# Second block: value products of a whole head per key block, probabilities left unnormalised, and their reciprocals multiplied into the gate

## The chip, the cores and the metric

The kernel runs on one core of one Trainium2 chip. The metric is the device time of one execution in microseconds. The kernel before was timed three times: 941.24, 942.96 and 945.05 us, median 942.96 us. Engines are named as in the profile: PE is TensorE, DVE is VectorE, ACT is ScalarE, POOL is GpSimd, and SP is the queue that issues the DMAs.

## The reference

One sequence of 512 positions and 1024 columns goes through two blocks. The first is retention and differential attention; the change does not touch it. The second has sixteen heads of 64 value columns: eight "a" heads (dilated windows, three patterns, here folded into one biased softmax over 512 keys) and eight "b" heads (latent attention, causal). Each head's output is normalised by its softmax sum, gated, and projected:

```
def dilated_pattern(q, k, v, rel_bias, window, dilation):
    ...
    m = jnp.max(s, axis=-1, keepdims=True)
    p = jnp.exp(s - m)
    den = jnp.sum(p, axis=-1)
    ...
    o = jnp.einsum('bnrhqk,bnkrhd->bnqrhd', p, vw) / den_q[..., None]

def latent_attention(...):
    ...
        p = jax.nn.softmax(s, axis=-1)
        return jnp.einsum('bhqk,bkhd->bqhd', p, v)

def hybrid_layer(...):
    ...
    mixed = jnp.concatenate([o_a * jax.nn.silu(z_a), o_b * jax.nn.silu(z_b)], axis=-1)
    out = jnp.matmul(mixed, w_out.astype(jnp.float32))
    return (x.astype(jnp.float32) + out).astype(x.dtype)
```

## The kernel before, in words

Every dense operand is held as a high part (rounded to fp32r) and a low part (the rest), and a product is three matmuls: high by high, low by high, high by low (mm3, lines 308 to 310). The high part is a copy on ACT, the low part a subtraction on DVE (split, lines 270 and 271). For streamed weights (Streamer, lines 138 and 140) the subtraction is on DVE, or on POOL for the keys in POOL_LO.

The attention of the second block walks 64 steps: 16 heads in the order a0 to a3, b0 to b7, a4 to a7, and four query tiles t of 128 positions each. Step s does this, in the order in which the PE instructions are written (PE runs in that order; the other engines' queues are ordered by a scheduler):
- probs(s): scores of query tile t against its t+1 key blocks, a score minimum on DVE (L1115), the exponential with its sum on ACT (L1118), the reciprocal of the sum and the scaling of the row by it on DVE (L1120, L1121);
- at t = 1 and t = 2 the queries and keys of the head four steps on are transposed and stacked (ready_q, ready_k); their tiles come from a ring of 12 (QK_BUFS), 6 for a pair of a heads, 4 for a b head;
- fill: dense work of the block (gates z, projections u, q, k, v, and the last projection "wo2") is dealt out so that PE has something to do while DVE and ACT work;
- probs_T(s - 2): the t+1 blocks of the row tile of two steps ago are transposed on PE (ppt), split into high (pTh, ACT) and low (pTl, DVE);
- fill again;
- weigh(s - 3): value products. For each of the t+1 key blocks three matmuls with 64 weight columns (v of this head, high or low) and 128 moving columns (one query tile of the transposed probabilities), all into one 64x512 PSUM tile per head (oTp). After t = 3 ACT copies it (osb, L1147), and after every second head mix_in multiplies by the gate (mtmp, L1153) and splits the result (mixh, mixl) for the last projection, L1185 to L1194.

PSUM: two tiles for the transposes (ps_t), two for the scores, three for dense work, one for the value products. A table of relative biases (tb) comes back from DRAM for every a head. The loop over steps is L1252 to L1262.

Of the kernel before, what the change touches and what calls it, by code (L numbers as in the profile page):

```python
# [11 lines left out]
F32 = mybir.dt.float32  # L12
# [8 lines left out]
S = 512  # L21
# [29 lines left out]
POOL_LO = frozenset(FILL)  # L51

QK_BUFS = 12
P_BUFS = 4
# [102 lines left out]
def two_block_kernel(ctx: ExitStack, tc: tile.TileContext, A: dict, out: bass.AP):  # L157
# [123 lines left out]
    def stack_q(pool, src, col):  # L281
        out = []
        for own, other in halves:
            t = pool.tile([P, S], F32R, name="qst", tag="qk", bufs=QK_BUFS)
# [6 lines left out]
    def stack_k(pool, src):  # L291
        out = []
        for own, other in halves:
            hi = pool.tile([P, S], F32R, name="ksh", tag="qk", bufs=QK_BUFS)
            lo = pool.tile([P, S], F32R, name="ksl", tag="qk", bufs=QK_BUFS)
# [609 lines left out]
    with tc.tile_pool(name="work2", bufs=2) as wp, tc.tile_pool(name="work2c", bufs=1) as wp1:  # L905
# [19 lines left out]
        for tp in range(2):  # L925
            cn = wp.tile([P, 2, 256], F32, name="cn", tag="tb")
            ck = wp.tile([P, 2, 160], F32, name="ck", tag="p", bufs=4)
# [62 lines left out]
        def mla_kv(half, out):  # L990
            (kh, kl), = st.get(f"ukv{half}")
            k = wp.tile([P, NT, 4, 96], F32, name="mk", tag="tm", bufs=4)
            vh = wp.tile([P, NT, 4, 64], F32R, name="mvh", tag="vh")
            vl = wp.tile([P, NT, 4, 64], F32R, name="mvl", tag="vl")
            for tt in range(NT):
# [3 lines left out]
                split(vh[:, tt], vl[:, tt], ps[:, :, 64:128])  # L999
# [11 lines left out]
            out.append((k, vh, vl))  # L1011

        def mla_prep(nm, src, h):
# [3 lines left out]
            hi = wp.tile([P, S], F32R, name=nm + "h", tag="qk", bufs=QK_BUFS)  # L1017
            lo = wp.tile([P, S], F32R, name=nm + "l", tag="qk", bufs=QK_BUFS)
# [35 lines left out]
        def dil_v(g):  # L1054
            vh = wp.tile([P, NT, 256], F32R, name="avh", tag="vh")
            vl = wp.tile([P, NT, 256], F32R, name="avl", tag="vl")

            def done(tp, ps):
                split(vh[:, 2 * tp : 2 * tp + 2, :], vl[:, 2 * tp : 2 * tp + 2, :], ps)

            yield from dense_TM_steps(st.get(f"v_a{g}"), done)
            v_a[g] = (vh, vl)

        def dil_prep(nm, i):
# [3 lines left out]
            return stack_q(wp, flat(pt), gcol[:, 18:19]) if nm == "q_a" else stack_k(wp, flat(pt))  # L1068
# [27 lines left out]
        def values_of(kind, h):  # L1096
            if kind == "b":
                _, vh, vl = kv_b[h // 4]
                return vh[:, :, h % 4, :], vl[:, :, h % 4, :]
            vh, vl = v_a[h // 4]  # L1100
            cv = slice(64 * (h % 4), 64 * (h % 4) + 64)
            return vh[:, :, cv], vl[:, :, cv]

        def probs(kind, h, t):
# [8 lines left out]
            p = wp.tile([P, S], F32, name="p", tag="p", bufs=4)  # L1113
# [182 lines left out]
```

## Time and profile before

| | |
|---|---|
| median of three runs | 942.96 us |
| profiled execution: its time / its span | 943.44 us / 941.4 us |
| PE busy | 918.0 us (98%), 5109 matmuls |
| DVE busy | 557.1 us (59%) |
| ACT busy | 452.8 us (48%) |
| POOL busy | 207.6 us (22%) |
| granted TensorE clock, mean | 0.993 of full speed |

PE's busy share is an upper reading: the ends of pipelined matmuls are modelled, so the distance between two starts tells what one costs. The attention of the second block runs from about 709 to 925 us. The shares of the whole span say little about it, so the rows below take it by stretch.

### The profile page before, as it was taken

The numbers are of one execution on the slowest core, as the hardware profiler recorded it, in microseconds if no ns is written. First come the engines' busy times: TensorE is split into PE (matmuls) and PEld (weight loads), VectorE is DVE, ScalarE is ACT, GpSimd is POOL, SyncE is SP. The second block draws the span as 40 slices with busy tenths as digits, with TensorE's granted clock in tenths as the row PEclk, the third lists the DMA queues.
The fourth block names the chain that finished last, engine by engine and source line by source line (L and its number), as shares of the span: only waits on it lengthen the run. The fifth ranks groups of instructions, "written<-read, shape, count | busy, mean of one in ns | idle before, by whom it ended". The sixth has DMA issues, their size and how long they took to land.

```text
span 941.4 us, 13693 instructions
## 1 busy us (share of the span) xinstructions
PE 918.0 (98%) x5109; PEld 778.2 (83%) x5109; DVE 557.1 (59%) x1222; ACT 452.8 (48%) x923; POOL 207.6 (22%) x234
## 2 busy tenths in 40 slices
PE   8999999999999999999999999999998989999998
PEld 5788887777888888888888888888997778999886
DVE  5434332428764655667765445444649897678884
ACT  5322231235555645666565432233546667666650
POOL 2001100107110223312310000032248453341100
PEclk8999999999999999999999999999999999999999
DMA  5575031211434433222432224544323221211412
GB/s 207 140 232 172 23 112 45 89 41 49 137 121 135 130 128 90 90 85 63 136 115 66 86 90 156 172 137 146 103 83 96 56 80 46 68 46 46 155 47 90
DMA packets 70241, 96.72 MB, mean 103 GB/s; under 512 B 5351, under 2 KB 46199, under 8 KB 70176
## 3 DMA queue, kind: packets, MB, share of 16 engines
q1 hardware_dynamic: 70176, 95.86, 32.6%
q8 instruction: 40, 0.66, 0.3%
q14 instruction: 25, 0.20, 0.1%
HBM read 87.43 MB, written 11.03 MB: 105 GB/s over the span
## 4 chain that ended last, share of the span: by engine, by line
PE 87%; DVE 6%; DMA 3%; ACT 2%; POOL 1%; issue 1%; SPq 0%; ACTq 0%
PE dps L308 9%; PE dps L310 9%; PE dps L309 9%; PE tps L308 7%; PE tps L310 7%; PE tps L309 7%; PE aps L308 2%; PE aps L309 2%; PE aps L310 2%; DMA wr<-in_w_in_dram 2%; PE dop L719 2%; PE ppt L1127 2%; PE ops L308 2%; PE yps L310 2%; PE yps L308 2%; PE yps L309 2%
## 5 line engine op out<-in xcount | busy, mean ns | idle before, releaser
L140 DVE TENSOR_TENSOR wl<-wr,wh 128x1024 fp32r<-128x1024 f32 (+2 forms) x115 | 141.8, 1234 | 117.7 <-ACT wh L138 113.8
L138 ACT ACTIVATE wh<-wr 128x1024 fp32r<-128x1024 f32 (+1 forms) x132 | 137.7, 1043 | 153.0 <-DMA wr<-in_w_in_dram 53.2
L308 PE MATMUL dps<-h1h,wh 128*128 128x512 f32 x320 | 128.3, 401 | 0.0
L310 PE MATMUL dps<-h1h,wl 128*128 128x512 f32 x320 | 125.1, 392 | 0.0
L309 PE MATMUL dps<-h1l,wh 128*128 128x512 f32 x320 | 125.0, 390 | 0.0
L308 PE MATMUL tps<-wh,h1h 128*128 128x512 f32 x256 | 104.5, 409 | 4.9 <-ACT dqn L387 2.5
L310 PE MATMUL tps<-wh,h1l 128*128 128x512 f32 x256 | 103.0, 403 | 0.0
L309 PE MATMUL tps<-wl,h1h 128*128 128x512 f32 x256 | 102.0, 399 | 0.3 <-DVE wl L140 0.2
L310 PEld LDWEIGHTS dps<-h1h,wl 128*128 128x128 f32 x320 | 60.1, 188 | 13.1
L308 PEld LDWEIGHTS dps<-h1h,wh 128*128 128x128 f32 x320 | 60.1, 188 | 12.3 <-ACT vv L491 0.5
L309 PEld LDWEIGHTS dps<-h1l,wh 128*128 128x128 f32 x320 | 60.2, 188 | 11.4
L308 PEld LDWEIGHTS tps<-wh,h1h 128*128 128x128 f32 x256 | 49.1, 192 | 17.4 <-ACT dqn L387 4.2
L309 PEld LDWEIGHTS tps<-wl,h1h 128*128 128x128 f32 x256 | 49.0, 191 | 11.1 <-DVE wl L140 1.6
L310 PEld LDWEIGHTS tps<-wh,h1l 128*128 128x128 f32 x256 | 49.0, 191 | 10.9 <-DVE h1l L271 0.3
L308 PE MATMUL aps<-wh,h2h 128*128 128x256 f32 x192 | 56.9, 296 | 0.0
L309 PE MATMUL aps<-wl,h2h 128*128 128x256 f32 x192 | 54.2, 282 | 0.0
L310 PE MATMUL aps<-wh,h2l 128*128 128x256 f32 x192 | 54.2, 282 | 0.0
L140 POOL TENSOR_TENSOR wl<-wr,wh 128x1024 fp32r<-128x1024 f32 (+2 forms) x17 | 38.1, 2245 | 38.7 <-ACT wh L138 31.0
L690 DVE CUSTOM_DVE_ANT_0 p<-sp,tb 128x128 f32<-128x128 f32 (+3 forms) x64 | 29.0, 488 | 29.4 <-PE sp L305 29.3
L1118 ACT ACTIVATE p<-p,nm 128x128 f32<-128x128 f32 (+1 forms) x64 | 35.7, 557 | 21.9 <-DVE nm L1115 21.6
L693 ACT ACTIVATE p<-p,nm 128x128 f32<-128x128 f32 (+3 forms) x64 | 35.5, 556 | 15.0 <-DVE nm L690 14.7
L253 POOL TENSOR_TENSOR gnrs<-gnrs,mhalf 128x8 f32<-128x8 f32 x24 | 41.8, 1748 | 1.7
(288 smaller groups left out, 2202.0 us busy)
## 6 DMA issues: line engine op xcount, KB each, us to landing
wr<-in_w_in_dram SPq DMA_DIRECT2D x92, 512.0 KB, 3.6
wr<-in_w_out_dram SPq DMA_DIRECT2D x16, 512.0 KB, 3.9
wr<-in_ret_w_o_dram SPq DMA_DIRECT2D x8, 512.0 KB, 3.4
wr<-in_diff_w_o_dram SPq DMA_DIRECT2D x8, 512.0 KB, 3.7
rep_dram<-rev_dram SPq DMA_DIRECT2D x8, 320.0 KB, 5.3
y_dram<-my SPq DMA_DIRECT2D x8, 256.0 KB, 2.0
my<-y_dram SPq DMA_DIRECT2D x8, 256.0 KB
m_dram<-mth SPq DMA_DIRECT2D x8, 256.0 KB, 3.3
```

Source lines behind the costliest of these rows:

```text
L138: nc.scalar.activation(hi, raw, AF.Copy)
L140: eng.tensor_tensor(lo, raw, hi.bitcast(F32), op=ALU.subtract)
L253: nc.gpsimd.tensor_tensor(dst, dst, mhalf[:, :n], op=ALU.pow)
L308: nc.tensor.matmul(ps, lh, rh, start=start, stop=False)
L309: nc.tensor.matmul(ps, lh, rl, start=False, stop=False)
L310: nc.tensor.matmul(ps, ll, rh, start=False, stop=stop)
L690: nc.vector.tensor_tensor_reduce(p[:, :n], sp[:, :n], tables[head][:, S - n : S], scale=-1.0, scalar=3.0e38, op0=ALU.add, op1=ALU.min, acc ...
L693: nc.scalar.activation(p[:, :n], p[:, :n], AF.Exp, scale=-1.0, bias=nm, accum_out=den)
L719: nc.tensor.matmul(o_ps[:, t, :], aT[:, kt, :], vd[head // 4][:, kt, hc], start=kt == 0, stop=kt == t)
L1118: nc.scalar.activation(p[:, :n], p[:, :n], AF.Exp, scale=-1.0, bias=nm, accum_out=den)
L1127: nc.tensor.transpose(pt[:, kt, :], p[:, kt * P : (kt + 1) * P], ident)
```

## The change

Where the kernel before multiplies per query tile, the kernel after waits for a head's four tiles and multiplies per key block. The high and low halves of v lie side by side in one tile of 128 columns per head, so one matmul gives both products, the high one in PSUM rows 0 to 63, the low one in rows 64 to 127; it runs once with the high and once with the low part of the probabilities, over all query tiles that see the key block (512, 384, 256, 128 columns). The transposed probabilities of a head are laid out so that these columns lie together (13 blocks, two tiles per head). ACT copies rows 64 to 127 out, DVE adds them to rows 0 to 63.

The rows of probabilities are no longer scaled. The four sums of a head are gathered, doubled, inverted and written to DRAM; they come back as a row of 512 spread over 64 partitions, and for every pair of heads POOL multiplies the gate by the two rows. Besides, the low parts of the weights wo2_0 and wo2_1 move from DVE to POOL, the ring of query and key tiles in this block has 9 tiles instead of 12, that of the row tiles p 3 instead of 4, and a doubling in the query norm of the b heads goes.

```diff
-POOL_LO = frozenset(FILL)
+POOL_LO = frozenset(FILL + ("wo2_00", "wo2_01", "wo2_10", "wo2_11"))
+QK_BUFS2 = 9
...
                 ss = stat.tile([P, 8], F32, name="uss", tag="uss")
...
-                nc.vector.tensor_scalar(ss[:, 4:8], ss[:, 4:8], 2.0, None, op0=ALU.mult)
                 rs = stat.tile([P, 8], F32, name="urs", tag="urs")
-                rstd(rs, ss, 8, 1.0 / 64)
+                for c4, w in ((slice(0, 4), 64), (slice(4, 8), 32)):
+                    nc.gpsimd.tensor_scalar(rs[:, c4], ss[:, c4], 1.0 / w, EPS, op0=ALU.mult, op1=ALU.add)
+                nc.gpsimd.tensor_tensor(rs, rs, mhalf[:, :8], op=ALU.pow)
...
-                split(vh[:, tt], vl[:, tt], ps[:, :, 64:128])
+                split(v[:, tt, :, 0:64], v[:, tt, :, 64:128], ps[:, :, 64:128])
...
-            p = wp.tile([P, S], F32, name="p", tag="p", bufs=4)
+            p = wp.tile([P, S], F32, name="p", tag="p", bufs=3)
...
-            den = stat.tile([P, 1], F32, name="den", tag="den")
-            nc.scalar.activation(p[:, :n], p[:, :n], AF.Exp, scale=-1.0, bias=nm, accum_out=den)
-            rd = stat.tile([P, 1], F32, name="rd", tag="rd")
-            nc.vector.reciprocal(rd, den)
-            nc.vector.tensor_scalar(p[:, :n], p[:, :n], rd, 0.5, op0=ALU.mult, op1=ALU.mult)
+            if t == 0:
+                den_now[0] = stat.tile([P, NT], F32, name="den4", tag="den4")
+            den = den_now[0]
+            nc.scalar.activation(p[:, :n], p[:, :n], AF.Exp, scale=-1.0, bias=nm, accum_out=den[:, t : t + 1])
+            if t == NT - 1:
+                nc.vector.tensor_scalar(den, den, 2.0, None, op0=ALU.mult)
+                rd = stat.tile([P, NT], F32, name="rd", tag="rd")
+                nc.vector.reciprocal(rd, den)
+                nc.sync.dma_start(rd_dram[h // 2 + (4 if kind == "b" else 0), h % 2].rearrange("t p -> p t"), rd)
             return p
...
         def probs_T(p, t):
+            if t == 0:
+                pT_now[:] = [wp.tile([P, 13, P], F32R, name=f"pT{a}", tag="pT") for a in "hl"]
             pt = ps_t.tile([P, NT, P], F32, name="ppt", tag="t")
...
+            to = slice(t, 4 * t + 1, 3)
+            split(pT_now[0][:, to, :], pT_now[1][:, to, :], pt[:, : t + 1, :])
...
-        def weigh(kind, h, t, pT):
...
-            for i in range(t + 1):
-                mm3(o_ps[0][:, cq], vh[:, i, :], vl[:, i, :], pT[0][:, i, :], pT[1][:, i, :], i == 0, i == t)
-            if t == NT - 1:
-                j = h % 2
-                nc.scalar.activation(o_sb[kt][64 * j : 64 * j + 64, :], o_ps[0], AF.Copy)
+        def weigh(kind, h, pT):
...
+            for i in range(NT):
+                for a in range(2):
+                    nc.tensor.matmul(o_ps[:, i * P :], v[:, i, :], flat(pT[a][:, 4 * i : 3 * i + 4, :]),
+                                     start=i == 0 and a == 0, stop=i == NT - 1 and a == 1)
+            j = h % 2
+            half = wp.tile([64, S], F32, name="ohalf", tag="th", bufs=1)
+            nc.scalar.activation(half, o_ps[64:128], AF.Copy)
+            nc.vector.tensor_tensor(o_sb[kt][64 * j : 64 * j + 64, :], o_ps[0:64], half, op=ALU.add)
+            if j == 0:
+                rdb[kt] = wp.tile([P, S], F32, name="rdb", tag="rdb", bufs=1)
+            nc.sync.dma_start(rdb[kt][64 * j : 64 * j + 64, :],
+                              rd_dram[kt, j].rearrange("t p -> (t p)")[None, :].to_broadcast([64, S]))
+            if j == 1:
+                mix_in(kt)

         def mix_in(kt):
+            nc.gpsimd.tensor_tensor(zws[kt], zws[kt], rdb.pop(kt), op=ALU.mult)
             tmp = wp.tile([P, S], F32, name="mtmp", tag="th", bufs=1)
             nc.vector.tensor_tensor(tmp, zws[kt], o_sb[kt], op=ALU.mult)
...
             fill(s, 0.5)
+            if s > LAG:
+                pT = pT_of.pop(s - LAG - 1)
+                if steps[s - LAG - 1][2] == NT - 1:
+                    weigh(*steps[s - LAG - 1][:2], pT)
             if 0 <= s - LAG < n_steps:
                 pT_of[s - LAG] = probs_T(p_of.pop(s - LAG), steps[s - LAG][2])
             fill(s, 1.0)
-            if s > LAG:
-                weigh(*steps[s - LAG - 1], pT_of.pop(s - LAG - 1))
```

Lines of the kernel after stand 1 to 20 lines further down than the same lines before. Up to the first value matrix of the second block the order on all engines is the same.

PE before, where the fifth b head's value products of the first query tile stand ahead of the sixth's first scores (aps is dense work, sp are scores; names with numbers are weight tiles):

```order
L308 MATMUL aps<-wh_0_7823,h2h 128x256
L309 MATMUL aps<-wl_0_7824,h2h 128x256
L310 MATMUL aps<-wh_0_7823,h2l 128x256
L308 MATMUL oTp<-pTh,mvh 64x128
L309 MATMUL oTp<-pTl,mvh 64x128
L310 MATMUL oTp<-pTh,mvl 64x128
L308 MATMUL sp<-kh,qh 128x128
L309 MATMUL sp<-kl,qh 128x128
L310 MATMUL sp<-kh,ql 128x128
```

PE after, at the place where a b head's whole product now stands, behind the first half of the step's dense work and ahead of the next transpose (ppt):

```order
L310 MATMUL aps<-wl_1_7572,h2h 128x256
L311 MATMUL aps<-wh_1_7571,h2l 128x256
L1155 MATMUL oTp<-pTh,mv 128x512
L1155 MATMUL oTp<-pTl,mv 128x512
L1155 MATMUL oTp<-pTh,mv 128x384
L1155 MATMUL oTp<-pTl,mv 128x384
L1155 MATMUL oTp<-pTh,mv 128x256
L1155 MATMUL oTp<-pTl,mv 128x256
L1155 MATMUL oTp<-pTh,mv 128x128
L1155 MATMUL oTp<-pTl,mv 128x128
L1139 MATMUL ppt<-ident,p 128x128
L309 MATMUL aps<-wh_1_7571,h2h 128x256
```

The three short products ahead of the scores are gone, as are those of the three other tiles; eight long ones stand once per head, and the score matmuls follow dense work.

DVE before, in the b heads (L1115 is the score minimum with its read-out, L1120 and L1121 the reciprocal and the scaling, zw a gate, ql a query's low part):

```order
L1115 ISA p,nm<-sp,dist 128x128
L1115 ISA nm 128x1
L384 SCALAR_TENSOR_TENSOR zw<-gth,zps 128x512
L1120 RECIPROCAL rd<-den 128x1
L271 TENSOR_TENSOR pTl<-ppt,pTh 128x384
L1121 TENSOR_SCALAR p<-p,rd 128x128
L1115 ISA p,nm<-sp,dist 128x256
L1115 ISA nm 128x1
L275 SCALAR_TENSOR_TENSOR ql<-mpt,gcol,qh 96x512
L1120 RECIPROCAL rd<-den 128x1
L1121 TENSOR_SCALAR p<-p,rd 128x256
```

DVE after, at the end of a pair of b heads (L1118 is the score minimum there, osb the sum of the two halves, mtmp the gated output, kl a key's low part, mv a value's):

```order
L1009 TENSOR_TENSOR mk<-mk,rrs 128x4x64
L272 TENSOR_TENSOR mv<-ups,mv 128x4x64
L1160 TENSOR_TENSOR osb<-oTp,ohalf 64x512
L272 TENSOR_TENSOR pTl<-ppt,pTh 128x128
L1171 TENSOR_TENSOR mtmp<-zw,osb 128x512
L1118 ISA p,nm<-sp,dist 128x512
L1118 ISA nm 128x1
L1006 TENSOR_REDUCE rss<-usq 128x4
L272 TENSOR_TENSOR mixl<-mtmp,mixh 128x512
```

The reciprocal and the scaling have left the steps; the sum of the halves and the gated output stand in front of the next score minimum.

POOL before, around the first weights of v_a1 (gnrs is a norm, wl a weight's low part):

```order
L252 TENSOR_SCALAR gnrs<-gns 128x8
L253 TENSOR_TENSOR gnrs<-gnrs,mhalf 128x8
L140 TENSOR_TENSOR wl_0_8150<-wr_0_8145,wh_0_8149 128x1024
L140 TENSOR_TENSOR wl_1_8154<-wr_1_8147,wh_1_8153 128x1024
L252 TENSOR_SCALAR gnrs<-gns 128x8
L253 TENSOR_TENSOR gnrs<-gnrs,mhalf 128x8
L252 TENSOR_SCALAR gnrs<-gns 128x8
L253 TENSOR_TENSOR gnrs<-gnrs,mhalf 128x8
L252 TENSOR_SCALAR gnrs<-gns 128x8
```

POOL after, around the first weights of the last projection (zw<-zw,rdb is the gate product; rdb is the row from DRAM):

```order
L253 TENSOR_SCALAR gnrs<-gns 128x8
L254 TENSOR_TENSOR gnrs<-gnrs,mhalf 128x8
L1169 TENSOR_TENSOR zw<-zw,rdb 128x512
L141 TENSOR_TENSOR wl_0_8139<-wr_0_8134,wh_0_8138 128x1024
L141 TENSOR_TENSOR wl_1_8143<-wr_1_8136,wh_1_8142 128x1024
L253 TENSOR_SCALAR gnrs<-gns 128x8
L254 TENSOR_TENSOR gnrs<-gnrs,mhalf 128x8
L298 COPY ksh<-ksh 64x512
```

The gate product and the two weight subtractions of wo2_00 have moved in among the norms, and the norm and the key copy (ksh) behind them wait for all three.

## Rows read from the trace of the kernel before

**Rows 1.** Busy time by stretch: us, engines busy (count), granted clock, DMA share, GB/s
```profile
715.00:780.00 65.00, 57.98 (x387) 48.72 (x386) 59.33 (x181) 42.68 (x106) 34.64 (x36) 0.97 0.24 68
730.00:735.00 5.00, 3.62 (x19) 3.14 (x20) 4.21 (x10) 2.75 (x8) 1.93 (x4) 0.66 0.36 105
780.00:920.00 140.00, 139.85 (x1110) 126.64 (x1109) 111.46 (x295) 89.72 (x207) 34.45 (x31) 1.00 0.22 69
```

**Rows 2.** TensorE's waits between 715 and 780 us: total, times, longest
```profile
PE ppt L1127 <- DVE pTl L271: 2.9, 2, 1.7
PE apt L1067 <- DVE pTl L271: 2.2, 1, 2.2
PE ppt L1127 <- DVE qst L286: 2.0, 1, 2.0
```

**Rows 3.** The same view for the value products alone (PE, weight loads, ACT)
```profile
780.00:920.00 140.00, 27.49 (x336) 26.22 (x335) 6.49 (x11) 1.00 0.22 69
```

**Rows 4.** Timeline of TensorE, 800 to 811 us: start, duration, instruction
```profile
800.17 0.22 PE L308 MATMUL oTp<-pTh,mvh 128*64 128x128 f32 x1
...
800.88 0.44 PE L308 MATMUL sp<-kh,qh 96*128 96x512 f32 x1
801.17 0.40 PE L309 MATMUL sp<-kl,qh 96*128 96x512 f32 x1
801.40 0.40 PE L310 MATMUL sp<-kh,ql 96*128 96x512 f32 x1
...
803.44 0.27 PE L308 MATMUL sp<-kh,qh 96*128 96x128 f32 x1
803.55 0.28 PE L309 MATMUL sp<-kl,qh 96*128 96x128 f32 x1
...
806.77 0.28 PE L309 MATMUL sp<-kl,qh 96*128 96x256 f32 x1
806.89 0.28 PE L310 MATMUL sp<-kh,ql 96*128 96x256 f32 x1
...
810.03 0.34 PE L309 MATMUL sp<-kl,qh 96*128 96x384 f32 x1
810.21 0.34 PE L310 MATMUL sp<-kh,ql 96*128 96x384 f32 x1
```

**Rows 5.** Stretch view of VectorE's line 1121 alone
```profile
715.00:780.00 65.00, 10.20 (x19) 0.97 0.24 68
```

**Rows 6.** Timeline of GpSimd and VectorE, 711 to 714 us
```profile
711.80 2.43 POOL L140 TENSOR_TENSOR wl<-wr,wh 128x1024 fp32r<-128x1024 f32 x1
...
713.08 1.25 DVE L1121 TENSOR_SCALAR p<-p,rd 128x128 f32<-128x128 f32 x1
```

**Rows 7.** Groups by line and form: busy us, mean ns | idle before, releasers
```profile
L140 POOL TENSOR_TENSOR wl<-wr,wh 128x1024 fp32r<-128x1024 f32 x14 | 33.6, 2402 | 36.1 <-ACT wh L138 28.4 <-PE mpt L1016 7.6
...
L881 POOL TENSOR_TENSOR xg<-x,g 128x512 f32<-128x512 f32 x8 | 12.0, 1494 | 85.1 <-DMA x<-in_x_dram 64.1 <-DVE x L878 21.0
...
L1120 DVE RECIPROCAL rd<-den 128x1 f32<-128x1 f32 x64 | 10.0, 157 | 9.0 <-ACT p L1118 8.7
...
L298 DVE TENSOR_TENSOR ksl<-apt,ksh 64x512 fp32r<-64x512 f32 x8 | 5.5, 688 | 0.5 <-ACT ksh L296 0.3
...
L296 ACT ACTIVATE ksh<-apt 64x512 fp32r<-64x512 f32 x8 | 4.7, 592 | 3.6 <-PE apt L1067 3.0 <-DVE ksl L298 0.5
```

**Rows 8.** Timeline of VectorE and TensorE, 809 to 812 us
```profile
809.49 0.68 DVE L271 TENSOR_TENSOR pTl<-ppt,pTh 128x512 fp32r<-128x512 f32 x1
...
811.87 0.27 PE L1127 MATMUL ppt<-ident,p 128*128 128x128 f32 x1
```

**Rows 9.** Waits of SP's queue over the span: total, times, longest
```profile
SPq L125 <- POOL wl L140: 105.0, 14, 17.2
...
SPq L595 <- DMA rev_dram<-rv: 2.6, 1, 2.6
```

**Rows 10.** DMA issues by line: count, size each, median us to landing
```profile
dec<-in_c_kdecay_dram SPq DMA_DIRECT2D x8, 128.0 KB, 7.1
```

More of the change, by code (lines that the diff above doesn't have):

```diff
@@ L279, in two_block_kernel, with stack_q @@
     halves = ((slice(0, 64), slice(64, 128)), (slice(64, 128), slice(0, 64)))
-    def stack_q(pool, src, col):
+    def stack_q(pool, src, col, bufs=QK_BUFS):
         out = []
         for own, other in halves:
-            t = pool.tile([P, S], F32R, name="qst", tag="qk", bufs=QK_BUFS)
+            t = pool.tile([P, S], F32R, name="qst", tag="qk", bufs=bufs)
             nc.scalar.activation(t[own], src[own], AF.Copy, scale=col[own])
@@ L1010, in mla_kv @@
                 yield 3 * S
-            out.append((k, vh, vl))
+            out.append((k, v))
         def mla_prep(nm, src, h):
@@ L1054, in dil_v @@
         def dil_v(g):
-            vh = wp.tile([P, NT, 256], F32R, name="avh", tag="vh")
-            vl = wp.tile([P, NT, 256], F32R, name="avl", tag="vl")
+            v = wp.tile([P, NT, 4, P], F32R, name="av", tag="v")
             def done(tp, ps):
-                split(vh[:, 2 * tp : 2 * tp + 2, :], vl[:, 2 * tp : 2 * tp + 2, :], ps)
+                for i in range(2):
+                    split(v[:, 2 * tp + i, :, 0:64], v[:, 2 * tp + i, :, 64:128],
+                          ps[:, i].rearrange("p (h w) -> p h w", w=64))
             yield from dense_TM_steps(st.get(f"v_a{g}"), done)
-            v_a[g] = (vh, vl)
+            v_a[g] = v
         def dil_prep(nm, i):
@@ L1096, in values_of @@
         def values_of(kind, h):
[L1097 to L1102, printed above, removed]
+            v = kv_b[h // 4][1] if kind == "b" else v_a[h // 4]
+            return v[:, :, h % 4, :]
+        den_now = [None]
+        rd_dram = dram.tile([8, 2, NT, P], F32, name="rd_dram")
         def probs(kind, h, t):
@@ L1127, in probs_T @@
                 nc.tensor.transpose(pt[:, kt, :], p[:, kt * P : (kt + 1) * P], ident)
-            ph = wp.tile([P, NT, P], F32R, name="pTh", tag="pTh")
-            pl = wp.tile([P, NT, P], F32R, name="pTl", tag="pTl")
-            split(ph[:, : t + 1, :], pl[:, : t + 1, :], pt[:, : t + 1, :])
-            return ph, pl
-        mix, zws, o_sb, o_ps = {}, {}, {}, {}
-        def weigh(kind, h, t, pT):
-            kt = h // 2 + (4 if kind == "b" else 0)
-            if t == 0:
-                o_ps[0] = ps_o.tile([64, S], F32, name="oTp", tag="o")
-                if h % 2 == 0:
-                    o_sb[kt] = oT_pool.tile([P, S], F32, name="osb", tag="o")
-            vh, vl = values_of(kind, h)
-            cq = slice(t * P, (t + 1) * P)
-            for i in range(t + 1):
-                mm3(o_ps[0][:, cq], vh[:, i, :], vl[:, i, :], pT[0][:, i, :], pT[1][:, i, :], i == 0, i == t)
-            if t == NT - 1:
-                j = h % 2
-                nc.scalar.activation(o_sb[kt][64 * j : 64 * j + 64, :], o_ps[0], AF.Copy)
-                if j == 1:
-                    mix_in(kt)
+            to = slice(t, 4 * t + 1, 3)
@@ new lines, in probs_T @@
+            split(pT_now[0][:, to, :], pT_now[1][:, to, :], pt[:, : t + 1, :])
+            return list(pT_now)
+        mix, zws, o_sb, rdb = {}, {}, {}, {}
+        def weigh(kind, h, pT):
+            kt = h // 2 + (4 if kind == "b" else 0)
+            if h % 2 == 0:
+                o_sb[kt] = oT_pool.tile([P, S], F32, name="osb", tag="o")
+            v = values_of(kind, h)
+            o_ps = ps_o.tile([P, S], F32, name="oTp", tag="o")
+            for i in range(NT):
[12 more added lines that the diff above has]
+                mix_in(kt)
```

19 lines of the change are left out of this document (10 added, 9 removed).

## Prediction

> **What bounds the kernel now.** I read the busy time by stretch first, because the change touches only the attention of the second block. Between 780 and 920 us TensorE is busy 139.85 of 140 us, VectorE 111.46, ScalarE 89.72 and GpSimd 34.45: there the time is TensorE's own instructions and nothing else. Between 715 and 780 us TensorE is busy 57.98 of 65 us and VectorE 59.33, and the granted clock falls to 0.66 (a mix of the 1.2 and the 2.4 GHz level) from 730 to 735 us [rows 1]. Second come TensorE's waits in that earlier stretch: they add up to 7.1 us, and all end on VectorE, on the low half of the transposed probabilities (pTl) or on a query stack (qst) [rows 2]. So the reader is to see two regimes: 65 us in which VectorE's queue is late, then 140 us in which only removed TensorE work counts.
>
> **TensorE: value products.** Per head the kernel before runs 10 key blocks of 3 matmuls, each with 64 weight columns and 128 moving columns. All 16 heads make 480; 336 of them lie between 780 and 920 us [rows 3]. Twelve in a row start at 800.17 and give way at 800.88, so one costs 0.71 / 12 = 0.059 us, a head 1.78 us, all heads 28.4 us. The new form is 4 key blocks of 2 matmuls with 128 weight columns and 512, 384, 256 and 128 moving columns. The trace has all four sizes with 128 weight columns: 512 takes 801.17 to 801.40, about 0.235 us; 384 takes 810.03 to 810.21, 0.18; 256 takes 806.77 to 806.89, 0.12; 128 takes 803.44 to 803.55, 0.11 [rows 4]. The last is nearly twice the 0.059 us of the 64-column form, so a short matmul is paced by its weights and the new form pays that for its last pair. Per head 2 x (0.235 + 0.18 + 0.12 + 0.11) = 1.29 us, all heads 20.6 us: 7.8 us less.
>
> A second saving hides in the order. A score matmul that follows the short products starts its successor late: 800.88 to 801.17 is 0.29 us for 512 columns where 0.235 is usual [rows 4]. Now it follows a dense matmul instead at three of four steps, 48 x 0.05 = 2.4 us. Together 10.2 us; by the count of products 7.1 us between 780 and 920, 2.7 us between 715 and 780, 0.4 us after 920.
>
> **VectorE between 715 and 780 us.** The scaling of the probabilities (L1121) goes: 19 there, 10.20 us [rows 5]. One of them shows why it is dear: 128 columns at 713.08 take 1.25 us and end as GpSimd's weight subtraction of 711.80 to 714.23 ends [rows 6]. The per-step reciprocals go too, 19 x 0.157 = 3.0 us [rows 7]. New are, per head, a doubling and a reciprocal of 4 columns (no such row; I take the 0.157 us of the 1-column one, bounds 0.08 and 0.6 change little), 4.75 heads x 0.31 = 1.5 us, and the sum of the two halves, a 64x512 operation with one input in PSUM, 0.688 us by the key split [rows 7], four times: 2.8 us. VectorE comes to 59.3 - 10.2 - 3.0 + 1.5 + 2.8 = 50.4 us. TensorE's floor there is 58.0 - 2.7 = 55.3 us, less 3.62 busy us x 0.34 = 1.2 us if the clock no longer falls: 54.1 us. Idle that remains lies between 0 and 7.0 us; VectorE would still be 88% busy and its queue is in order, so I take half, 3.5 us. The stretch becomes 57.6 us, 7.4 us less.
>
> Elsewhere VectorE's and ScalarE's gains cost and give nothing, since TensorE hides them. ScalarE's copy out of the product changes place, not size. The subtraction of the last projection's weights moves from VectorE to GpSimd, 2.40 us each there [rows 7]: six, and GpSimd was busy 34 of 140 us. If that cover went, the projection would wait at most one of them, 2.4 us.
>
> **New waits.** (a) The whole product of a head now waits for its fourth transposed block and stands half a step nearer to it. At 809.49 pTl starts, 0.68 us long; the point where the product now stands is 811.87, and nine short products (0.54 us) no longer lie ahead of it: 1.16 us to spare [rows 8]. I price it at 0, at most 2 us over the heads of the early stretch.
> (b) Nine query and key buffers instead of twelve. A pair of the first kind needs six; at three places (second, third and fourth pair) the last key tiles wait until the previous head's fourth scores are done. From there ScalarE's copy, 0.592 us, and VectorE's subtraction, 0.688 us [rows 7], must free the transposes' PSUM tile, with about 0.7 us of dense matmuls as cover: 0.6 us each, 1.8 us. Bounds 0 and 3 x 1.28 = 3.9 us.
> (c) The reciprocals go to DRAM and come back as a row on SP's queue, in order among the weight loads; GpSimd multiplies the gate by the row (1.494 us by the 128x512 product [rows 7]) and VectorE's gated output waits for that, with the score minima and pTl of the next steps queued behind it. Nearest rows: a write that the queue waited for before reading it back, 2.6 us, and the landing of a 64-partition row broadcast, 7.1 us [rows 9, 10]. Together 2.6 + 7.1 + 1.5 = 11.2 us. A step is 140 us over 336 / 7.5 = 44.8 steps, 3.1 us; from the reciprocal to the gated output there are three steps and the two operations after the product, less the softmax ahead, about 9 us. So it is late by about 2 us at the 8 gated outputs, and TensorE sees what exceeds its 1.16 us to spare. Bounds: 0, and 8 x 1.0 = 8 us. The 7.1 us were measured with rows issued back to back, so I take 2 us.
>
> **Sum.** Profiled run: 943.44 us, of which the span is 941.4. 7.1 + 7.4 + 0.4 - 1.8 - 2.0 = 11.1 us less: span 930.3, time 932.3; the profiled run lay 0.5 us over the median of 942.96, so 932 us. The tail is not lengthened: after the last product 18 dense matmuls of 0.235 us, 4.2 us, stand before the first that needs the last output, and the longer chain (copy 0.59, sum 0.69, gate 0.69, split 0.62) takes 2.6 us.
>
> **Rivals.**
> 1. Slower: VectorE stands at the gated output because the row is stuck on SP. For: SP waited 105.0 us in 14 waits for GpSimd's weight subtractions, 7.5 us each [rows 9], and the row is queued behind such loads, while more subtractions move to GpSimd. Against: the loads are rarely waiting just when the row is due, and the two order lists put the transfers ahead of the waiting load at most places. If 4 of 8 outputs are hit, 4 x (7.5 + 2 - 1.16) = 33 us against 13.1 us of gain: about 963 us. It turns the sign from 3.3 us of lost TensorE time per hit place at 4 places.
> 2. The idle stays. GpSimd gets 8 gate products and 6 subtractions, 8 x 1.494 + 6 x 2.40 = 26.4 us of long operations, and one such held a VectorE operation for a microsecond [rows 6]. If each holds VectorE for half its length and half of that reaches TensorE, 6.6 us come back: 938.5 us. For: that row. Against: the operation that was held there is the one that goes. The Trainium skill, "SBUF — State Buffer", section "SBUF: two separate sides", states the rule behind it: GpSimd and VectorE share one port pair under an exclusive lock, which a VectorE operation with two SBUF inputs needs too, and the later one blocks. By that rule the gated output and the norms can still be held, and the row of 1.25 us agrees for the scaling.
> 3. More: VectorE's queue clears wholly and nothing new waits. 941.4 - 10.2 - 7.0 - 1.2 = 923.0, about 924.5 us.
> 4. The change doesn't do what it says: the repeated weight load paces the long products as well. Then a product of 256 or more columns would cost more than a dense matmul of that size; the dense rows of 128 weights speak against it, and at 0.29 us for 512 [rows 4] only 1.8 us would be lost. It is inside the range.
>
> **How the numbers follow.** Forecast with 927 to 937 us: 0.56. Rival 3: 0.17. Rival 2 with what lies between 937 and 942: 0.17. Rival 1: 0.10. The range 923 to 942 leaves out rival 1 and the far end of rival 3. About 0.5% is what a measurement here tells from no change: below 938.2 us is faster, above 947.7 slower. Faster 0.56 + 0.17 + 0.10 = 0.83, same 0.09, slower 0.08.
>
> **What would show it.** Right: products of 0.235, 0.18, 0.12 and 0.11 us, some 20 us in all; TensorE's waits between 715 and 780 us halved and the clock at 1.00 in 730 to 735; VectorE without the scaling; at most 2 us of waits by a transpose at the three pair changes. Wrong: TensorE idle behind VectorE after each gated output, with VectorE's gate product waiting for GpSimd and GpSimd for the row; weights (wl) of the last projection arriving late; or an early stretch that stays at 65 us although VectorE is lighter.

## The result and the profile after

The kernel after takes 1024.99 us (median of four runs, 1022.85 to 1025.54), the kernel before 942.1 us beside it: ratio 1.0864, 95% interval 1.0845 to 1.0883. The forecast was 932 us; the change costs 82.9 us (82 against the earlier median of 942.96).

Busy time of the kernel after by stretch (columns: us, then PE, weight loads, DVE, ACT and POOL busy with their counts, granted clock, DMA share, GB/s), to be held against [rows 1]:

```profile
690.00:715.00 25.00, 25.00 (x209) 25.00 (x208) 11.71 (x22) 12.51 (x25) 10.28 (x9) 1.00 0.29 89
715.00:780.00 65.00, 51.87 (x257) 42.90 (x256) 45.47 (x130) 38.13 (x92) 40.77 (x51) 0.92 0.22 59
780.00:850.00 70.00, 50.65 (x261) 42.30 (x260) 37.88 (x100) 34.76 (x82) 25.60 (x23) 0.83 0.24 57
850.00:930.00 80.00, 63.42 (x453) 60.86 (x452) 42.10 (x98) 38.95 (x88) 25.95 (x20) 0.85 0.28 49
930.00:1024.00 94.00, 68.70 (x305) 54.78 (x303) 44.03 (x95) 28.19 (x65) 13.80 (x11) 0.89 0.24 80
```

No engine is full any more. VectorE is lighter (45.47 of 65 us where it had 59.33), but TensorE is idle for 334 - 259.64 = 74.4 us of these 334, and the granted clock, 0.97 to 1.00 before, is 0.83 to 0.92 of full speed from 715 us on, a mix of its two levels (1.2 and 2.4 GHz).

Waits of all engines from 690 us on (total, times, longest), which answer to [rows 2]:

```profile
POOL zw L1169 <- DMA rdb<-rd_dram: 117.5, 8, 29.9
...
PE ppt L1139 <- DVE pTl L272: 42.4, 9, 11.5
...
DVE mk L1009 <- POOL rrs L254: 23.8, 4, 13.0
DVE mtmp L1171 <- POOL zw L1169: 22.2, 3, 8.0
...
DVE aqn L395 <- POOL gnrs L254: 15.8, 4, 11.4
```

Read in the order of cause: GpSimd waits for the row, 117.5 us in eight gate products; VectorE waits for norms (rrs, gnrs) and for the gate (zw), all of them GpSimd's; TensorE waits for VectorE. The DMA queue's own waits (over the span) and two of the DMA lines (count, size, median us to landing), against [rows 9] and [rows 10], say why the row is late:

```profile
SPq L1163 <- DMA rd_dram<-rd: 159.4, 16, 12.1
SPq L126 <- POOL wl L141: 44.4, 7, 9.8
```

```profile
rdb<-rd_dram SPq DMA_DIRECT2D x16, 128.0 KB, 5.0
...
rd_dram<-rd SPq DMA_DIRECT2D x16, 2.0 KB, 9.3
```

At each of the 16 reads the queue stands 10 us until the reciprocals' write has landed. One such place in the timeline of the kernel after (start, duration, instruction, in brackets the idle time before it and what ended it):

```profile
815.31 0.17 DVE L1127 RECIPROCAL rd<-den 128x4 f32<-128x4 f32 x1
815.62 1.46 SPq L1128 DMA_DIRECT2D rd_dram<-rd  x1
828.56 0.45 SPq L1163 DMA_DIRECT2D rdb<-rd_dram  x1
832.84 1.26 POOL L1169 TENSOR_TENSOR zw<-zw,rdb 128x512 f32<-128x512 f32 x1 [13.47 <-DMA rdb<-rd_dram]
834.46 1.01 POOL L254 TENSOR_TENSOR rrs<-rrs,mhalf 128x4 f32<-128x4 f32 x1
835.50 2.56 DVE L1009 TENSOR_TENSOR mk<-mk,rrs 128x256 f32<-128x256 f32 x1 [13.03 <-POOL rrs L254]
839.49 0.90 PE L1139 MATMUL ppt<-ident,p 128*128 128x128 f32 x3 [11.54 <-DVE pTl L272]
840.04 0.78 PE L309 MATMUL zps<-h2h,wh 128*128 128x512 f32 x1
840.62 0.63 PE L310 MATMUL zps<-h2l,wh 128*128 128x512 f32 x1
841.04 0.63 PE L311 MATMUL zps<-h2h,wl 128*128 128x512 f32 x1
```

From reciprocal to gate product it is 17.5 us: 12.9 from write to read, 4.3 for the read (14.3 to 18.6 us over the eight pairs). A key norm (rrs) queued behind the gate product on GpSimd holds VectorE 13.03 us, with the pTl that TensorE needs behind it. After its 11.54 us of idle time TensorE starts dense matmuls 0.42 us apart instead of 0.23 until 842.75.

From 715 us on TensorE has eight gaps of 5.2 to 11.5 us. Six of them end on this chain from row to GpSimd to VectorE. The other two, at 790.45 and 944.11, end on transfers that were issued only after the queue had stood at a read: weights issued at 779.23 behind the read of 778.68, and rows for the last projection (part) at 936.25 behind that of 935.76. ScalarE and VectorE waited for them:

```profile
785.66 1.06 ACT L139 ACTIVATE wh<-wr 128x1024 fp32r<-128x1024 f32 x1 [5.67 <-DMA wr<-in_w_in_dram]
942.33 0.69 DVE L1209 TENSOR_TENSOR part<-part,ops 128x512 f32<-128x512 f32 x1 [9.84 <-DMA part<-x_dram]
```

What the DMA engines do meanwhile is in the same stretch view, at the first write (issued at 730.64, read issued at 742.22):

```profile
730.00:731.00 1.00, 1.00 (x9) 0.96 (x8) 1.00 (x7) 0.99 (x4) 0.77 (x2) 1.00 0.00 0
731.00:732.00 1.00, 1.00 (x6) 0.79 (x5) 1.00 (x1) 0.68 (x1) 1.00 (x1) 1.00 0.25 2
732.00:733.00 1.00, 0.41 (x2) 0.00 (x0) 1.00 (x1) 0.00 (x0) 1.00 (x1) 1.00 0.00 0
...
738.00:742.00 4.00, 4.00 (x23) 3.44 (x22) 3.90 (x7) 2.33 (x6) 2.54 (x2) 1.00 0.00 0
```

The 512 pieces of 4 bytes keep the DMA engines busy for a quarter of one microsecond (DMA share 0.25); then nothing moves for ten, until the write counts as landed.

The products themselves are near the forecast. Timeline of TensorE in the kernel after, against [rows 4]:

```profile
809.56 0.39 PE L1155 MATMUL oTp<-pTh,mv 128*128 128x512 f32 x1
...
809.79 0.39 PE L1155 MATMUL oTp<-pTl,mv 128*128 128x512 f32 x1
...
810.02 0.33 PE L1155 MATMUL oTp<-pTh,mv 128*128 128x384 f32 x1
810.19 0.34 PE L1155 MATMUL oTp<-pTl,mv 128*128 128x384 f32 x1
```

The starts are 0.23 and 0.17 us apart (0.235 and 0.18 forecast); the eight end at 810.78, 1.22 us a head against 1.29.

### The profile page after: what moved, and what is told of

Read it like the earlier page. It is cut to its first block, busy times and chain, and to the rows that moved or that the text cites. A ratio compares the mean times of both kernels' runs of the same rounds, so it can differ in the third digit from the quotient of the medians.

```text
span 1023.8 us, 12999 instructions
## 1 busy us (share of the span) xinstructions
PE 938.4 (92%) x4757; PEld 784.4 (77%) x4757; DVE 537.0 (52%) x1132; ACT 454.5 (44%) x927; POOL 236.5 (23%) x256
## 4 chain that ended last, share of the span: by engine, by line
PE 69%; DMA 14%; DVE 8%; POOL 3%; issue 3%; ACT 2%; SPq 0%; POOLq 0%; DVEq 0%; ACTq 0%
PE dps L309 9%; PE dps L311 9%; PE dps L310 9%; PE tps L309 6%; PE tps L311 6%; PE tps L310 6%; DMA rd_dram<-rd 6%; DMA rdb<-rd_dram 2%; DMA wr<-in_w_in_dram 2%; PE dop L720 2%; PE yps L310 1%; PE yps L311 1%; PE yps L309 1%; PE aps L309 1%; PE aps L310 1%
## 5 line engine op out<-in xcount | busy, mean ns | idle before, releaser
L141 DVE TENSOR_TENSOR wl<-wr,wh 128x1024 fp32r<-128x1024 f32 (+2 forms) x109 | 133.5, 1225 | 117.0 <-ACT wh L139 113.2
L1139 PE MATMUL ppt<-ident,p 128*128 128x128 f32 x160 | 32.6, 308 | 42.4 <-DVE pTl L272 42.4
L309 PEld LDWEIGHTS tps<-wh,h1h 128*128 128x128 f32 x256 | 48.7, 190 | 17.7 <-ACT dqn L388 4.5
L141 POOL TENSOR_TENSOR wl<-wr,wh 128x1024 fp32r<-128x1024 f32 (+2 forms) x23 | 52.9, 2307 | 38.1 <-ACT wh L139 31.2
L1139 PEld LDWEIGHTS ppt<-ident,p 128*128 128x128 f32 x160 | 21.9, 156 | 50.4 <-DVE pTl L272 29.6
L311 PEld LDWEIGHTS tps<-wh,h1l 128*128 128x128 f32 x256 | 48.7, 190 | 11.5 <-DVE h1l L272 0.3
```

The lines of the kernel that those rows point to most:

```text
L141: eng.tensor_tensor(lo, raw, hi.bitcast(F32), op=ALU.subtract)
L309: nc.tensor.matmul(ps, lh, rh, start=start, stop=False)
L311: nc.tensor.matmul(ps, ll, rh, start=False, stop=stop)
L1139: nc.tensor.transpose(pt[:, kt, :], p[:, kt * P : (kt + 1) * P], ident)
```

## Experiments

T1 is the theory above (the row's late landing), T2 says GpSimd has too much to do, T3 that the product's form, its place or the smaller rings cost. Each run was timed beside the kernel before (943.4 to 944.1 us in the four groups of runs).

**The row left out.** Edit to the kernel after:

```diff
-                nc.sync.dma_start(rd_dram[...].rearrange("t p -> p t"), rd)
-            nc.sync.dma_start(rdb[kt][64 * j : 64 * j + 64, :], rd_dram[kt, j]...)
-            nc.gpsimd.tensor_tensor(zws[kt], zws[kt], rdb.pop(kt), op=ALU.mult)
```

> The row is left out whole: no write of the reciprocals, no read back, no gate product with it, so the outputs are not normalised. All else is the changed kernel. Theory T1 (the row's write of 512 four-byte pieces lands 9 to 12 us after its issue, the sync queue stands at the read, GpSimd at the gate product, VectorE and TensorE behind GpSimd, and TensorE's clock falls in the gaps): all of the loss goes and the products' gain shows, 922 to 935 us. Rival T2 (GpSimd is overloaded by the work that was moved to it, 6 weight subtractions of 2.4 us and 8 gate products): of the added GpSimd work of about 25 us the subtractions, 14.5 us, stay, so more than half of the 82 us stays, 965 to 1000 us. Rival T3 (the whole-head product, or nine query and key buffers, makes TensorE wait): 1000 to 1025 us.

946.19 us, ratio 1.0034 (1.0019 to 1.0048). Nearly all of the loss is the row's, and T3 falls as its cause; T2 falls for the moved subtractions here, and for the gate products in the run below that reads but does not write. But the gain of the products does not show. Its trace has the reason: the first matmul of the second block's latent projection (cps) starts at 652.1 us, in the kernel before at 644.6. 7.5 us are lost in the first block, which the change does not touch.

**Rows that are ready.**

```diff
-                              rd_dram[kt, j].rearrange("t p -> (t p)")[None, :].to_broadcast([64, S]))
+                              rev_dram[kt : kt + 1, :S].to_broadcast([64, S]))
```

> The reads of the row stay in number, size and place (16 of 128 KB to 64 partitions), but read a row that lay in memory long before (of the bias tables), so no read waits for a write; the writes of the reciprocals stay too, the gate product too. Left out by this: the right values of the row. T1: the 159 us of the sync queue's standing at the reads go, the gate product finds its row about 4.5 us after the read's issue (as in the profile after); 925 to 942 us. T2: nothing of GpSimd's work is gone, so 990 to 1025 us. T3: 1000 to 1025 us. If the 4-byte writes themselves slow other transfers, it lies between, 945 to 980 us.

971.25 us, ratio 1.0299 (1.0282 to 1.0316). Without any wait for the write, 25 us over the run without the row stay: the case "between". In its trace a 512 KB weight tile needs 10.3 us to land (median of 14); 3.6 us in the run below that reads but does not write.

**Pieces of 512 bytes.**

```diff
+            nc.tensor.transpose(rT[:NT, :], rd, ident)
+            nc.vector.tensor_copy(rr, rT[:NT, :])
+            nc.sync.dma_start(rd_dram[kt, j], rr)
```

> The whole computation; the reciprocals of a head are transposed on TensorE to 4 partitions of 128, copied to SBUF on VectorE and written as 4 pieces of 512 bytes instead of 512 of 4 bytes, one step later than before; the read, the gate product and their places stay. T1 with the piece size as the cause: the write lands in 2 to 3 us, before the read is due, the standing at the reads falls from 10 us each to under 2 us; 928 to 945 us. If instead any write that is read back on this queue costs its 10 us: 1005 to 1030 us. T2 and T3: 1000 to 1030 us.

964.95 us, ratio 1.0216 (1.0183 to 1.025): slower than forecast, but its queue no longer stands at the reads (waits of the DMA queue):

```profile
SPq L1171 <- DMA rd_dram<-rr: 15.3, 16, 1.7
```

1 us each where it was 10, and the read is issued 1.2 us after the write: the same 2 KB land within that time in four long pieces. Left over are the first block's loss, 18.3 us in which TensorE stands at the new transposes, and GpSimd's 41.0 us for the row.

**Side edits alone**, on the kernel before (POOL_LO, nine query and key buffers, three of p):

> The kernel before with only the side edits: the last projection's weight subtractions on GpSimd, nine query and key buffers, three probability buffers. T1: these are no part of the loss, 938 to 948 us. T2: the six subtractions on GpSimd carry a good part of it, 960 to 1000 us. T3 with the buffers as the cause: 960 to 1000 us, with TensorE's transposes waiting at the pair changes.

942.59 us, ratio 0.999 (0.998 to 0.9999): they cost nothing.

**128, 256 and 96 unused bytes**, on the kernel before:

```diff
+    pad = ctx.enter_context(tc.tile_pool(name="pad", bufs=1)).tile([P, 32], F32, name="pad")
+    nc.vector.memset(pad, 0.0)
```

> The kernel before with nothing but 128 unused bytes per partition ahead of the buffers of both blocks (with one memset to fill them), so that every later buffer lies 128 bytes higher in SBUF, where it lies in the changed kernel, whose 4-column denominators took a new place in the pool of small tiles. In the run without the row the first block, which the change does not touch, lost 7.5 us by the first matmul of the second block's latent projection (cps, 644.6 to 652.1 us), with 512-column matmuls following each other at 0.232 instead of 0.227 us. If the shift does that: cps starts at 650 to 653 us and the whole is 947 to 952 us. If it is something else in the changed program: cps at 644 to 645 us, 941 to 944 us.

> The kernel before with 256 unused bytes per partition ahead of the buffers of both blocks. The run with 128 bytes lost 11.6 us, nearly all of it in the first block (cps from 644.6 to 654.8 us). If only the place within 256 bytes counts (128 bytes apart is bad, 256 is the same as 0): 941 to 946 us, cps at 644 to 646 us. If any shift of these buffers against the weights' buffers, which do not move, costs: 950 to 957 us, cps at 650 us or later.

> The kernel before with 96 unused bytes instead, which puts the first buffer behind them at a multiple of 256 bytes (66816). If such a place is the best for TensorE's reads: 936 to 942 us. If it is as bad as 128 bytes: 952 to 957 us. If the reads care for nothing finer than 128 bytes: as the kernel before, 941 to 946 us.

128 bytes: 955.54 us, 1.0116 (1.0097 to 1.0136). 256 bytes: 944.55 us, 1.0012 (0.9998 to 1.0026). 96 bytes: 954.43 us, 1.0117 (1.0099 to 1.0135). The first blocks differ in pace: here 64 of the 192 matmuls of the mixing product in the kernel before, with 128 and with 256 bytes (shortest, median and longest ns; first and last start):

```profile
L308 PE MATMUL tps<-wh,mh x64: 389/389/473, 599.5 to 643.3; 128*128 128x512 f32 x64
```

```profile
L310 PE MATMUL tps<-wh,mh x64: 392/394/479, 608.5 to 653.4; 128*128 128x512 f32 x64
```

```profile
L310 PE MATMUL tps<-wh,mh x64: 389/389/473, 599.8 to 643.5; 128*128 128x512 f32 x64
```

The 192 take 1.1 us longer (0.006 us each) with 128 bytes, and the same with 256. The first buffer starts at byte 66720 in the kernel before (160 over a multiple of 256), 66848 in the one after (32 over), 66816 and 66976 with 96 and 256 bytes (0 and 160 over). So 160 bytes over a multiple of 256 is fast both times, and both other places are slow. (The addresses are those of the built programs. The buffers of the streamed weights lie lower and do not move.)

**The kernel after without the shift.**

```diff
-                den_now[0] = stat.tile([P, NT], F32, name="den4", tag="den4")
+                den_now[0] = stat.tile([P, NT], F32, name="den4", tag="den")
```

> The changed kernel, but its 4-column denominators take the place in the pool of small tiles that the 1-column ones have in the first block, so that no buffer moves. Nothing else differs. If the shift is a part of the 82 us by itself: cps at 644 to 646 us instead of 652, and 1012 to 1019 us in all. If the shift costs nothing by itself: 1023 to 1027 us.

998.83 us, ratio 1.0594 (1.0573 to 1.0615): one word is worth 26 us. cps starts at 644.0 instead of 652.2, so 8 us come from the first block. The other 18 come behind it, where from write to read the 16 rows now take 148 us together instead of 169 (by the issues of L1128 and L1163). Why a write lands sooner there was not tried; the buffer that it is written from moves with the shift, too.

**Row left out, no shift; and row read, but not written.**

> The changed kernel without the row (no write, read or gate product of it; the outputs are not normalised) and with the denominators in their old place, so that no buffer moves. With the 7.5 us of the shift gone from the run without the row (946.2 us): 936 to 941 us. If that run's lag had another cause: 944 us or more.

> No buffer moves; the row is read (16 reads of 128 KB) from tables that lay in memory long before, and multiplied into the gate on GpSimd, but the reciprocals are not written: the values of the row are left out. T1 (only the write and its order on the sync queue cost): 936 to 944 us. T2 (the reads of 64 copies and GpSimd's products cost): 950 to 965 us, near the 971 of the run with both writes and ready rows less the shift.

937.34 us, 0.9939 (0.9919 to 0.9959), and 941.98 us, 0.9984 (0.9966 to 1.0003). Without row and shift the change gains 6.2 us; reads and GpSimd's products cost 4.6, the writes with the waits for them 998.8 - 942.0 = 56.8.

**Written twice**, first to a row that nobody reads (no shift):

> The changed kernel with the denominators in their old place (998.8 us), each head's reciprocals written twice in pieces of 4 bytes, first to a row that nobody reads, then to the row that is read. If the landing of the 512 pieces sets the loss and it is a matter of their number: the sync queue stands some 17 us instead of 9 at each of the 16 reads and the whole is 1090 to 1140 us. If the landing is a fixed delay: 998 to 1010 us.

1112.38 us, ratio 1.1814 (1.1757 to 1.1871). Waits of the DMA queue:

```profile
SPq L1165 <- DMA rd_dram<-rd: 237.3, 15, 17.9
```

15.8 us a read, 8.7 (139.7 in 16) with one write: the delay is not a fixed one. That it goes by the pieces, not by the write, follows only together with the run of four pieces; whether by their number or by their size, no run separates.

**The row later.**

```diff
-            if j == 1:
-                mix_in(kt)
+            if j == 1:
+                late.append([kt, 0])   # read 3 steps on, mix_in 5 steps on
```

> The row goes the same way through memory, in pieces of 4 bytes, but is read three steps after the pair's product, and the gate product, the gated output and its split come two steps later still; the last pair's follow at once; the last projection's two parts start two and four steps later for it. No shift of the buffers. T1: the writes have landed before the sync queue comes to the read, and the row before GpSimd comes to the gate product, so only the last pair waits, some 10 us at the end: 940 to 955 us. If the 4-byte writes themselves disturb other transfers, or if GpSimd's work is the cause (T2): 965 us or more.

1001.9 us, ratio 1.061 (1.059 to 1.063). That did not test T1: only TensorE's order is written out, and the planner put the reads right behind the writes as before (the queue stands 149.7 us at them). The second try made the read wait for the probabilities of a later step:

```diff
+                        nc.scalar.activation(rdb[e[0]][:, :1], p[:, :1], AF.Copy)
```

> As the version with the late row, whose reads the planner had put right behind the writes all the same, but the row's buffer is first touched by ScalarE after the probabilities of the second step behind the pair's product, which the read must await; so the reads stand some 15 us behind the writes in the sync queue too, and each head's row has a memory buffer of its own. Nothing is left out of the computation, no buffer moves. T1: the standing at the reads (140 us) and at the gate products (103 us) falls below a third, only the last pair's is exposed: 943 to 962 us. If the writes themselves hold other work up: 975 us or more.

990.01 us, ratio 1.0502 (1.0463 to 1.0541). The queue now stands at one write only (9.4 us), and GpSimd still waits 72.6 us for rows. Two reads issued from 786.02, just behind a later head's write of 784.68, and a weight tile of 512 KB issued at 789.93, in the stretch view:

```profile
785.00:786.00 1.00, 1.00 (x8) 0.82 (x7) 0.18 (x2) 0.71 (x4) 0.00 (x0) 1.00 0.25 2
...
787.00:790.00 3.00, 3.00 (x19) 2.57 (x18) 1.29 (x4) 2.18 (x5) 2.40 (x1) 1.00 0.05 3
790.00:793.00 3.00, 3.00 (x21) 2.69 (x20) 1.72 (x4) 2.11 (x5) 0.00 (x0) 1.00 0.10 8
...
796.00:797.00 1.00, 1.00 (x7) 0.88 (x6) 0.28 (x1) 1.00 (x4) 0.00 (x0) 1.00 0.96 301
```

They trickle at 3 to 8 GB/s until some 10 us after the write, then rows and weights run at 301, and the gate product starts at 797.38. So it is not only the wait: what is issued behind such a write is slow too, as the weight tiles were with the ready rows.

**Products alone** (probabilities scaled as before, no row, no shift):

```diff
+            nc.vector.tensor_scalar(p[:, :n], p[:, :n], rd, 0.5, op0=ALU.mult, op1=ALU.mult)
```

> Products alone: the new whole-head products with 128 weight columns, but the probabilities are scaled on VectorE step by step as before, so there is no row and no gate product; the buffers do not shift. T1: no wait for a row; TensorE gains the products' 7 to 10 us where it is the bound, and loses again where VectorE, with the scaling and the sum of the halves (16 x 0.68 us), is late: 933 to 943 us. T3 (the product's place or form costs): 945 us or more.

950.2 us, ratio 1.0066 (1.0051 to 1.0082), slower than forecast and in the range of T3. The trace speaks for VectorE instead: with scaling and sums it is busy 60.35 of 65, 59.80 of 70 and 59.06 of 70 us up to 920, and TensorE waits 17.7 us for its pTl (rows of ppt, oTp and apt: 9.3, 5.4, 3.0), where it waits 9.5 us without row and shift (6.2, 2.3, 1.0). So here the new products pay only if the scaling leaves VectorE.

**The row made on TensorE**, no shift; then also the last weight subtractions on GpSimd:

```diff
+                    nc.gpsimd.tensor_copy(rx.rearrange("p t (j w) -> p t j w", w=64),
+                                          rd_now[0][:, :, :, None].to_broadcast([P, NT, 2, 64]))
...
+                    nc.tensor.transpose(rb[:, t, :], rx[:, t, :], ident)
+                nc.vector.tensor_tensor(zws[kt], zws[kt], flat(rb), op=ALU.mult)
```

> The whole computation without the trip through memory: GpSimd spreads the reciprocals of a pair to 128 columns per query block, TensorE transposes them (4 transposes a pair, 32 in all) just ahead of the pair's second product, and VectorE multiplies the gate by the row in PSUM. The denominators take the old place in the pool of small tiles, so nothing shifts. T1: what the run without the row took (946) less the 7.5 us of the shift, plus 32 x 0.11 to 0.27 = 3.5 to 8.6 us of transposes, part of it in idle time: 937 to 947 us, and no engine waits for a row. T2 (GpSimd's work): 960 us or more. If the shift is not the cause of the 7.5 us: 946 to 955 us.

> The version whose row is made on TensorE, with the two last weight subtractions of the last projection on GpSimd too. In the run without the row two of these (1.22 us each on VectorE) stood ahead of the last but one pTl; TensorE stood 2.0 us at the product and then ran at half pace to the end of the next dense group, and a lead of 5.0 us over the kernel before became a lag of 1.0. If that is where the end of the gain goes: 934 to 939 us. If GpSimd then brings these weights late, or the stall has another cause: 941 to 946 us.

941.18 us, 0.9967 (0.9953 to 0.9981), and 937.58 us, 0.9938 (0.9918 to 0.9957). The whole computation with the second takes 6 us less than the kernel before and 87 less than the one after; the row on TensorE costs 3.8 us (941.18 against 937.34 without a row; 2.6 us by the two ratios). The moved subtractions seem to give 3.6 back, but the two intervals overlap, and the two traces differ by 3.0 us already at the first score minimum (713.16 and 710.18), behind work that the edit does not touch.

## Why the prediction was wrong

**The step that failed is (c) of the new waits.** The write was priced at the 2.6 us of [rows 9], a transfer of a few long pieces; from its issue to the read's it takes 9.2 to 13.4 us, and doubling its pieces nearly doubles it. The terms 7.1 and 1.5 us were near (5.0 and 1.27). With 9 us available the row was to be 2 us late; the true chain takes 14.3 to 18.6 us, GpSimd stands at all eight gate products, and TensorE has a gap of 5.2 to 11.5 us near each, not 1 us. The Trainium skill, "DMA: Bandwidth & Descriptors", section "Anatomy of one DMA — SWDGE (gpsimd) path", gives a DMA that GpSimd issues about 2 us of fixed cost, most of it the receipt of the last byte. The writes here go by the sync queue, and no run tries the other path; in four pieces the write lies below that figure (1.2 us from write to read), in 512 pieces far above it, and the measurement decides.

**The place was rival 1's, its cause and price were not.** VectorE stands behind GpSimd, and GpSimd for the row. But between write and read the queue stands for the write and not for weights; only one load is issued in between (at 880.57), and the landing there is no longer. Loads ahead of the write may add to it: the two longest landings, 12.9 and 13.4 us, follow right behind a row read and two weight loads; that was not tried. And the price counted only the gated output: on GpSimd norms queue behind the gate product, so VectorE was held there for up to 13 us, TensorE's clock fell in the gaps (0.83 from 780 to 850 us), and loads behind the read came late. The row's whole way costs 998.8 - 937.3 = 61.5 us, GpSimd's products with it.

**A term was missing: where the buffers lie.** The new tag of the denominators moved every later buffer by 128 bytes: 26.2 us in the kernel after, 8.9 us without the row, 11.6 us in the kernel before. Nothing in the prediction looked for it. The parts add up: 61.5 and 26.2 less a gain of 6.2 make 81.5 of the 82.9 us.

**The gain was half; that rival 2's time fits is luck.** Without row and shift it is 6.2 us; the terms but (c) made 13.1. Rival 2's time of 938.5 us is near the 937.34, but its operations are not there: this run has no gate products, and the first weights of the last projection are loaded at 828.3 us, behind the early stretch. By the read-out of each step's score minimum (nm) this kernel led by 778.98 - 776.50 = 2.5 us at step 20, where 7.4 us were forecast for the early stretch. VectorE is busy 56.27 of its 65 us, where 50.4 were forecast for the work of one step less (20 score minima instead of 19). The sum took the length of the operations that stay as fixed. Three groups of VectorE between 715 and 780 us (busy us, mean ns, idle before), first of the kernel before, then of the one without row and shift:

```profile
L984 DVE TENSOR_TENSOR mq<-mq,urs 128x256 f32<-128x256 f32 x8 | 5.1, 642 | 0.0
...
L919 DVE TENSOR_TENSOR rab<-mq,rope_q 128x128 f32<-128x128 f32 x12 | 2.9, 282 | 0.0
L920 DVE TENSOR_TENSOR rab<-rab 128x64 f32<-128x64 f32 x6 | 2.9, 479 | 0.0
```

```profile
L986 DVE TENSOR_TENSOR mq<-mq,urs 128x256 f32<-128x256 f32 x8 | 6.9, 862 | 1.6 <-POOL urs L985 1.6
L920 DVE TENSOR_TENSOR rab<-mq,rope_q 128x128 f32<-128x128 f32 x12 | 5.2, 475 | 0.1
...
L921 DVE TENSOR_TENSOR rab<-rab 128x64 f32<-128x64 f32 x6 | 1.3, 217 | 0.0
```

The same work takes 4.1 us more in two groups and 1.6 us less in the third, while operations with an input in PSUM keep their length (pTl of 512 columns 680 and 692 ns, zw 680 and 686). The Trainium skill's rule that the prediction named for rival 2 ("SBUF — State Buffer", section "SBUF: two separate sides") agrees in kind: all inputs of these groups lie in SBUF. GpSimd is busy 39.35 us there instead of 34.64, with six weight subtractions of 1024 columns instead of four and two scalar operations per query norm instead of one; which of its operations these groups meet was not followed, so the rule is not shown as the cause. TensorE still stands 65 - 58.11 = 6.9 us there. From step 20 to steps 60 to 62 the kernel gained 6.0 to 8.0 us more; the forecast for TensorE's bound part was 7.1. Then, in its timeline:

```profile
901.42 1.22 DVE L141 TENSOR_TENSOR wl<-wr,wh 128x1024 fp32r<-128x1024 f32 x1
...
903.03 1.22 DVE L141 TENSOR_TENSOR wl<-wr,wh 128x1024 fp32r<-128x1024 f32 x1
...
904.76 0.69 DVE L272 TENSOR_TENSOR pTl<-ppt,pTh 128x512 fp32r<-128x512 f32 x1
905.50 0.50 PE L1154 MATMUL oTp<-pTl,av 128*128 128x512 f32 x1 [2.05 <-DVE pTl L272]
```

Two weight subtractions stand ahead of the head's last pTl. That is wait (a), priced at 0 with a bound of 2 us over the early stretch: 2.05 us late in the run, and then matmuls 0.43 us apart instead of 0.23 to 909.4, another 2. Of a lead of 10.4 us at step 62, 4.5 are left at step 63. Not all of that is the subtractions': with them on GpSimd (row on TensorE) TensorE still stands 0.88 us there, and the lead falls from 8.0 to 4.5 us. The run with the row on TensorE and the subtractions on VectorE has the same 2.04 us of idle time, keeps its clock, and falls from 4.9 to 0.5. So by the traces the move is worth about 1 us at this place, and the run with the moved subtractions came into its forecast range partly by the 3.0 us that lie ahead.

**Right were** the products' durations, the saving where TensorE is the bound, and that the moved subtractions cost nothing (run of the side edits). The same run shows nothing of wait (b), which was priced at 1.8 us with 0 as its lower bound. Rival 4 is excluded by the products' starts.

**Open:** why a shift of 128 bytes also lengthens the landing of the write, and how the 56.8 us split between standing and held transfers. An estimate for the latter: ready rows, 971.25, less 8.9 us for the shift as in the run without a row, are 20 us over the run that reads and does not write.

## What to carry to other kernels

Price a small write by its pieces, not by its bytes: look for a transfer of the same piece size, and if there is none, let the range hold it. A round trip through memory in in-order queues must be priced with all that stands behind each of its waits, on every engine that takes part, loads in the DMA queue included. When a change adds a small tile, compare where the large buffers start, before anything else is explained.

## What the runs showed of the hardware

- 512 pieces of 4 bytes to DRAM: a quarter of a microsecond of the DMA engines, 9.3 us to landing (median); without the shift the queue stands 8.7 us at the read, and 15.8 us with two such writes; the same bytes in four pieces 1.2 us from write to read. Transfers issued behind them are slow too (512 KB: median 10.3 us instead of 3.6).
- Matmuls of 512 columns run 0.006 us (2.5%) slower when the buffers of one operand start 32 or 0 bytes over a multiple of 256 instead of 160, with the streamed weights' buffers unmoved; over the first block 8 to 12 us. Which of the moved buffers counts was not separated.
- After an idle gap of 2.05 us TensorE's granted clock was 0.57 for the next 4 us (905.5 to 909.4, without row and shift); after one of 2.04 us at the same place of the kernel with the row on TensorE it was 1.00. So the length of the gap alone does not tell whether the clock falls. The stretch views of both, the first with 903.00 to 905.50 ahead of it, the second behind the matmul that ends its gap:

```profile
903.00:905.50 2.50, 0.46 (x1) 0.14 (x1) 2.45 (x5) 0.71 (x2) 0.00 (x0) 1.00 0.00 0
905.50:909.40 3.90, 3.90 (x13) 3.41 (x14) 0.88 (x2) 0.87 (x2) 0.00 (x0) 0.57 0.02 4
```

```profile
911.01 0.50 PE L1166 MATMUL oTp<-pTl,av 128*128 128x512 f32 x1 [2.04 <-DVE pTl L272]
```

```profile
911.00:915.00 4.00, 3.99 (x22) 3.41 (x22) 2.04 (x4) 0.87 (x2) 0.00 (x0) 1.00 0.00 0
```
